# A tap table made at the start of the program, its cosine and sine rows in two partition groups

## The chip, the core and the metric

The kernel runs on one core of a Trainium2 chip. A core has a matrix engine (TensorE, PE in the profile; PEld is its loading of weights), a vector engine (VectorE, DVE), an activation engine (ScalarE, ACT), a general engine (GpSimd, POOL) and a sync engine (SyncE, SP) whose queue issues most of the transfers. Each engine runs its own instructions in order, and they meet at semaphores. The metric is device time in microseconds of one execution, the median of several runs; less is better.

## The reference

Two layers run over 256 latent tokens and 256 context tokens of width 1024. Layer 0 mixes tokens with a Conformer convolution module, layer 1 with a bidirectional mLSTM, and each is followed by an MLP with squared ReLU. The change concerns the start of layer 0:

```python
u = modulate(h, sh1, sc1)          # h * (1 + sc1) + sh1
def conformer_conv(u, rows, w_pw1, b_pw1, w_dw, b_dw, ln_g, ln_b, w_pw2, b_pw2):
    a = u @ w_pw1 + b_pw1
    a = a[..., :CONV_DIM] * jax.nn.sigmoid(a[..., CONV_DIM:])
    ...
        a = dwconv(a, w_dw)         # 31 taps, per channel
    ...
    a = jax.nn.silu(layer_norm(a + b_dw, ln_g, ln_b))
    return a @ w_pw2 + b_pw2
```

The shift `sh1` and the scale `sc1` come from `silu(c) @ ada_w + ada_b`.

## The kernel before

Features lie on the partitions in eight tiles of 128, and both token streams together are 512 columns. A large product is made of three matmuls (`mm3`, L181, L184, L185): a weight is split into a rounded part `wh` and a residual `wl`, the activation into `u` and its residual, and three of the four products are summed. The split of weights is a cast on ACT (L150) and a subtraction on DVE (L151).

**The load time.** The first eight blocks run in a loop over f. `start0(f)` loads a block of modulation weights (`raw`, 1024 KB), a tile of x (256 KB) and a piece of the first convolution weights (`F`, 256 KB), and runs eight matmuls of 32 columns each on four column tiles of PE (L343). `start1(f)` folds their four partial sums with a small matrix `fold` (L351), adds the biases out of `vecs` (L637, L638), splits the weights and makes u and its residual (L600, L601, L603). `start2(f)` runs twelve matmuls into four accumulators `ps0`. While `pin` is set, PE keeps the order of the program. Until the first loads have landed PE runs matmuls on a tile of ones (`idle`, L175): 13, then 3, then 5.

**The convolution.** The 31 taps are applied in the frequency domain: rows of a are transformed by a matmul with a table `F0`, multiplied by the taps' spectrum `Hc` and `Hs` on DVE (L867, L868) and transformed back with `G1` and `G2` (L878). The tables are angles, made of iotas on POOL, which DVE reduces and turns into sines by a polynomial of twelve steps (L704 to L713), once over 384 columns (`F0`, `G1`, `G2`) and once over 256 (`WC`, `WS`). The spectrum is `taps` (L735 to L740): four f32 matmuls of 31 rows of `WC` or `WS` with the taps, two after each of the second and third column blocks of the main product (m = 1 and 2 of `pw1_next`), each result scaled by `cf` on ACT. All of this stands in a region of lower priority (L667 to L741), so that its DVE instructions fall between those of the loop and the product.

**What sets the order.** A scheduler puts each engine's instructions in order; instructions that were issued with `keep_in_program_order` stay as they are written, and `issue_after` puts one behind another. SP issues the loads in the order of its queue: first `vecs` (204 KB), then raw, x and F of each block; a load into a tile that is still read waits in the queue, with all that stands behind it.

Of the kernel before, what the change touches and what calls it, by code (L numbers as in the profile page):

```python
# [14 lines left out]
P = 128  # L15
# [56 lines left out]
def hybrid_kernel(ctx: ExitStack, tc: tile.TileContext, xT, vecs_d, wdw_d, ada0_w, ada_w, wg_d, pw1a, pw1, pw2, w1_0, w2_0,  # L72
# [49 lines left out]
    def VA(name):  # L122
        o, w = _OFF[name]
        return vecs[:, o:o + w]

    ident = con.tile([P, P], F32, name="ident")
    make_identity(nc, ident)
    ones = con.tile([P, P], F32, name="ones")
# [8 lines left out]
    fold = con.tile([P, 16], F32, name="fold")  # L137
    nc.vector.tensor_tensor(fold, ident[:, 0:16], ident[:, 32:48], op=ALU.add)
    for j in (2, 3):
        folded = nc.vector.tensor_tensor(fold, fold, ident[:, 32 * j:32 * j + 16], op=ALU.add).ins  # L140
# [16 lines left out]
    def split_w(src, make=None):  # L157
        n = src.shape[-1]
        if make is not None:
            his, los = [], []  # L160
            for i in range(0, n, T):
                his.append(make(F32R))
                los.append(make(F32R))
                split(his[-1], los[-1], src[:, i:i + T])
            return his, los
        hi = wp.tile([P, 1024], F32R, tag="wh", name=nm("wh"), bufs=NW)[:, :n]
        lo = wp.tile([P, 1024], F32R, tag="wl", name=nm("wl"), bufs=NW)[:, :n]
        anchors.append(split(hi, lo, src))
        return hi, lo
# [3 lines left out]
    def idle(ps, n):  # L173
        for _ in range(n):
            a = nc.tensor.matmul(ps[:, 0:P], ones, ones, start=True, stop=True)  # L175
            if pin[0]:
                tc.keep_in_program_order(a)
        return a.ins
# [149 lines left out]

    cs = con.tile([P, DT, 48], F32, name="cs")
    nc.vector.memset(cs, 0.0)  # L330
    sgc = con.tile([P, 2 * DT], F32, name="sgc")
    cc = vecs[:, _OFF["c_ctx"][0]:_OFF["c_ctx"][0] + 2 * DT]
    nc.scalar.activation(sgc, cc, AF.Sigmoid)
    for i in range(2):
        nc.vector.tensor_tensor(cs[:, :, 14 + i], sgc[:, i * DT:(i + 1) * DT], cc[:, i * DT:(i + 1) * DT], op=ALU.mult)
    ada = [con.tile([P, 48, 2], F32, name=f"ada{l}") for l in range(2)]

    mark_unit = [None]
# [270 lines left out]
    F = maker(padp, "F", 5)  # L609

    x, u = [], []
    KO0 = 4
    ps0 = [psum("cv" if m == 3 else "mm") for m in range(KO0)]
    sc1 = con.tile([P, 2, DT], F32, name="sc1p")
# [3 lines left out]

    def start0(f):
        t = X()  # L620
        raw = raw_load(ada0_w[f])
        nc.sync.dma_start(t, xT[f * P:(f + 1) * P, :])
        wr = F()
        nc.sync.dma_start(wr[:, :KO0 * P], pw1a[f])
        x.append(t)
        ps = psum("fl")[:, :2 * P]
        ada_mm(ps, [raw[:, kt * 2 * P:(kt + 1) * 2 * P] for kt in range(DT)])
        sb = F()[:, :2 * P]
        with tc.issue_after(folded):
            st[f] = wr, sb, nc.vector.tensor_copy(sb, ps).ins  # L630

    def start1(f):
        with tc.issue_after(st[f][2]):
            w = split_w(st[f][0][:, 0:KO0 * P])
        tr = ada_fold(st[f][1], 2 * P, tag="ln")
        with tc.issue_after(lastsub[0]):
            nc.vector.tensor_scalar(sh1[:, :, f], tr[:, 0:2], vecs[:, o0 + f:o0 + f + 1], None, op0=ALU.add)  # L637
            nc.vector.tensor_scalar(sc1[:, :, f], tr[:, 2:4], vecs[:, o0 + DT + f:o0 + DT + f + 1], 1.0,  # L638
                                    op0=ALU.add, op1=ALU.add)
        u.append((U(F32R), U(F32R)))  # L640
        affine_split(*u[f], x[f], sc1, sh1, f)
        st[f] = w

    def start2(f, ms):
        for m in ms:
            mm3(ps0[m], *kcol(st[f], m), *u[f], f == 0, f == DT - 1)

    pin[0] = Z.pin0
# [18 lines left out]

    later = tc.high_priority(-100)
    later.__enter__()
    foldg = con.tile([P, 16], F32, name="foldg")  # L670
# [3 lines left out]
    HL = L // 2  # L674
    ij = F()
    fj, jj = ij[:, 0:L], ij[:, L:2 * L]
    pc = padp.tile([P, 8], F32, name="pc")
    exact = dict(channel_multiplier=0, allow_small_or_imprecise_dtypes=True)
# [3 lines left out]
    p_, gt, fp, p15, ph1, ph2, cf, z0 = [pc[:, i:i + 1] for i in range(8)]  # L682
    nc.gpsimd.iota(p_, [[1, 1]], base=0, channel_multiplier=1, allow_small_or_imprecise_dtypes=True)
    nc.vector.tensor_scalar(gt, p_, float(HL), None, op0=ALU.is_gt)
    nc.vector.scalar_tensor_tensor(fp, gt, -float(HL), p_, op0=ALU.mult, op1=ALU.add)
    nc.vector.tensor_scalar(p15, p_, float(NTAP // 2), None, op0=ALU.subtract)
# [3 lines left out]
    nc.vector.tensor_scalar(z0, p_, 0.0, None, op0=ALU.is_equal)  # L690
    nc.vector.tensor_scalar(cf, p_, float(HL), None, op0=ALU.is_equal)
    nc.vector.tensor_tensor(cf, cf, z0, op=ALU.add)
    nc.vector.tensor_scalar(cf, cf, -1.0 / L, 2.0 / L, op0=ALU.mult, op1=ALU.add)
    tab = padp.tile([P, 5 * L], F32, name="tab")
    F0, G1, G2, WC, WS = [tab[:, i * L:(i + 1) * L] for i in range(5)]
    nc.vector.tensor_scalar(F0, fj, p_, None, op0=ALU.mult)
    nc.vector.tensor_scalar(G1, jj, fp, ph1, op0=ALU.mult, op1=ALU.add)
    nc.vector.tensor_scalar(G2, jj, fp, ph2, op0=ALU.mult, op1=ALU.add)
    nc.vector.tensor_scalar(WC, fj, p15, None, op0=ALU.mult)
    nc.vector.tensor_scalar(WS, fj, p15, -L / 4, op0=ALU.mult, op1=ALU.add)  # L700
    nc.vector.tensor_scalar(F0[:, HL + 1:L], F0[:, HL + 1:L], -L / 4, None, op0=ALU.add)
    for t_ in (tab[:, 0:3 * L], tab[:, 3 * L:5 * L]):
        tz, sq_ = [F()[:, :t_.shape[-1]] for _ in range(2)]
        nc.vector.tensor_scalar(tz, t_, 1.0 / L, MAGIC, op0=ALU.mult, op1=ALU.add)  # L704
        nc.vector.tensor_scalar(tz, tz, MAGIC, -float(L), op0=ALU.subtract, op1=ALU.mult)
        nc.vector.tensor_tensor(t_, t_, tz, op=ALU.add)
        nc.vector.scalar_tensor_tensor(tz, t_, -1.0, t_, op0=ALU.mult, op1=ALU.max)
        nc.vector.tensor_scalar(t_, tz, -1.0, L / 4, op0=ALU.mult, op1=ALU.add)
        nc.vector.tensor_tensor(sq_, t_, t_, op=ALU.mult)
        nc.vector.tensor_scalar(tz, sq_, SIN[5], None, op0=ALU.mult)  # L710
        for k in (4, 3, 2, 1):
            nc.vector.scalar_tensor_tensor(tz, tz, SIN[k], sq_, op0=ALU.add, op1=ALU.mult)
        nc.vector.scalar_tensor_tensor(t_, tz, SIN[0], t_, op0=ALU.add, op1=ALU.mult)  # L713

    def masked(name, zero):
        t = padp.tile([P, L], F32, name=name)
# [10 lines left out]
    bdw = padp.tile([P, D], F32, name="bdw")  # L727
    nc.sync.dma_start(bdw, wdw_d[NTAP:NTAP + 1, :].broadcast_to([P, D]))
    Hc, Hs = [padp.tile([P, D], F32, name=n_) for n_ in ("Hc", "Hs")]

    wds = [tmp("L")[:NTAP, :] for _ in range(2)]
    for h_ in range(2):
        nc.sync.dma_start(wds[h_], wdw_d[0:NTAP, h_ * 512:(h_ + 1) * 512])

    def taps(h_):  # L735
        wd = wds[h_]
        for t, w_ in ((Hc, WC), (Hs, WS)):
            ps = psum("ln")
            nc.tensor.matmul(ps, w_[:NTAP, :], wd, start=True, stop=True)
            nc.scalar.activation(t[:, h_ * 512:(h_ + 1) * 512], ps, AF.Identity, scale=cf)  # L740
    later.__exit__(None, None, None)  # L741


# [185 lines left out]
    def pw1_next(m, ps):  # L929
# [27 lines left out]
        if m == 8:  # L957
            for i, tag in enumerate("SLSL"):
                half.append(tmp(tag))
                nc.sync.dma_start(half[i], ada_w[0, 6 + ada_s2.n, 0, :, i * 512:(i + 1) * 512])  # L960
        if m == 10:
            pw2_raw.extend(raw_load(pw2[g, 0]) for g in range(2))
            for i in range(4):
# [1100 lines left out]
```

## Time and profile before

| | us |
|---|---|
| three timed runs | 1659.6, 1661.2, 1662.05 |
| median | 1661.2 |
| span of the profiled execution, first to last instruction | 1658.8 |
| PE busy in it | 1647.3 |
| DVE busy | 1042.7 |
| ACT busy | 730.4 |
| mean granted PE clock | 0.998 of full |

The time of the profiled execution itself, with what lies before and after its span, isn't listed. In rows of the timeline stand the start, the length, the engine, the line, the operation with what it writes and reads, how many are merged, and in brackets how long the engine had been idle and what ended that. In rows of the chain stand the start, the length and the work: it is followed back from the last instruction, at each step to what released it. Groups by line give the busy time in all, the mean of one in ns, and the idle time ahead of them.

### The profile page before, as it was taken

The page shows a single profiled execution, that of the slowest core. Times are in us where ns is not written, and L with a number is a line of the kernel's source. Part 1 is how long each engine was busy: PE and PEld are TensorE (multiplying, and loading weights), DVE is VectorE, ACT ScalarE, POOL GpSimd, SP SyncE. Part 2 cuts the span into 40 slices and gives each one's busy share as a digit, 9 for nine tenths or more (in the row PEclk, how much of TensorE's full clock was granted, in tenths as well). Part 3 has the DMA queues.
Part 4 walks back from the last instruction along what each step waited for, and adds up shares of the span by engine and source line. Part 5 has one row for each costly group of instructions (what it writes and reads, how often), then busy time and mean ns, then how long its engine had stood idle before and what let it go on. Part 6 is the DMA issues. An engine that isn't in the chain of part 4 may idle for free.

```text
span 1658.8 us, 22681 instructions
## 1 busy us (share of the span) xinstructions
PE 1647.3 (99%) x8824; PEld 1357.0 (82%) x8824; DVE 1042.7 (63%) x1875; ACT 730.4 (44%) x1174; POOL 14.3 (1%) x64
## 2 busy tenths in 40 slices
PE   9999999999999999999999999999999999999998
PEld 7665998888888998877787899888878888878887
DVE  6564895666535776762254753563489776776677
ACT  4313572232324475652133533442478654555453
POOL 0000000000000000000000000000000000000001
PEclk9999999999999999999999999999999999999999
DMA  9666223434424066557774852554466655675552
GB/s 359 229 213 239 96 71 116 163 123 147 137 102 153 1 225 204 184 194 272 282 255 145 301 179 80 178 190 151 147 227 219 212 211 202 242 283 186 178 186 93
DMA packets 80411, 305.80 MB, mean 184 GB/s; under 512 B 11854, under 2 KB 30066, under 8 KB 50352
## 3 DMA queue, kind: packets, MB, share of 16 engines
q1 hardware_dynamic: 57840, 288.06, 49.5%
q10 hardware_dynamic: 22464, 16.30, 3.0%
q8 instruction: 69, 1.13, 0.3%
q14 instruction: 38, 0.31, 0.1%
HBM read 286.47 MB, written 17.86 MB: 183 GB/s over the span
## 4 chain that ended last, share of the span: by engine, by line
PE 93%; DVE 4%; DMA 1%; ACT 1%; issue 1%; SPq 0%; DVEq 0%; ACTq 0%
PE mm L181 17%; PE mm L184 17%; PE mm L185 17%; PE mm L196 7%; PE mm L197 4%; PE mm L212 3%; PE mm L214 3%; PE mm L213 3%; PE cv L212 2%; PE fl L343 1%; PE cv L214 1%; PE cv L213 1%; DVE wl L151 1%; PE ln L181 1%; PE cv L878 1%; PE ln L184 1%
## 5 line engine op out<-in xcount | busy, mean ns | idle before, releaser
L151 DVE TENSOR_TENSOR wl<-raw,wh 128x1024 fp32r<-128x1024 f32 x344 | 418.5, 1221 | 248.1 <-ACT wh L150 246.5
L150 ACT CAST wh<-raw 128x1024 fp32r<-128x1024 f32 x344 | 358.6, 1051 | 463.3 <-PE mm L184 245.1
L184 PE MATMUL mm<-u,wh 128*128 128x512 f32 (+1 forms) x808 | 292.2, 362 | 0.2 <-DVE u L603 0.2
L181 PE MATMUL mm<-u,wh 128*128 128x512 f32 (+1 forms) x680 | 244.1, 360 | 0.0
L185 PE MATMUL mm<-u,wl 128*128 128x512 f32 (+1 forms) x680 | 241.5, 356 | 0.0
L184 PEld LDWEIGHTS mm<-u,wh 128*128 128x128 f32 x808 | 153.0, 189 | 23.3 <-issue 1.0
L181 PEld LDWEIGHTS mm<-u,wh 128*128 128x128 f32 x680 | 128.8, 190 | 24.9 <-issue 6.3
L185 PEld LDWEIGHTS mm<-u,wl 128*128 128x128 f32 x680 | 128.8, 190 | 17.9
L212 PE MATMUL mm<-wh,xl 128*128 128x512 f32 x256 | 101.2, 395 | 0.9 <-ACT wh L150 0.8
L181 PE MATMUL mm<-xm,wh 128*128 128x512 f32 x256 | 101.0, 395 | 0.0
L213 PE MATMUL mm<-wh,xl 128*128 128x512 f32 x256 | 100.0, 391 | 0.0
L185 PE MATMUL mm<-xm,wl 128*128 128x512 f32 x256 | 99.7, 389 | 0.0
L214 PE MATMUL mm<-wl,xl 128*128 128x512 f32 x256 | 99.4, 392 | 0.1
L181 PE MATMUL mm<-hid,wh 128*128 128x512 f32 (+1 forms) x256 | 93.3, 364 | 0.0
L185 PE MATMUL mm<-hid,wl 128*128 128x512 f32 (+1 forms) x256 | 92.8, 363 | 0.0
L184 PE MATMUL mm<-hid,wh 128*128 128x512 f32 (+1 forms) x256 | 92.8, 363 | 0.0
L196 PE MATMUL mm<-x,wh 128*128 128x512 f32 x232 | 81.1, 398 | 0.0
L184 PE MATMUL mm<-qq,wh 128*128 128x272 f32 x256 | 73.9, 289 | 0.0
L181 PE MATMUL mm<-qq,wh 128*128 128x272 f32 x256 | 73.5, 288 | 0.0
L185 PE MATMUL mm<-qq,wl 128*128 128x272 f32 x256 | 73.5, 288 | 0.0
L196 PE MATMUL mm<-u,wh 128*128 128x512 f32 x192 | 68.6, 399 | 0.0
L1120 DVE SCALAR_TENSOR_TENSOR x<-mm,ada,x 128x256 f32<-128x256 f32 x64 | 28.5, 479 | 62.4 <-PE mm L185 62.4
(537 smaller groups left out, 3245.2 us busy)
## 6 DMA issues: line engine op xcount, KB each, us to landing
raw<-w SPq DMA_DIRECT2D x64, 1024.0 KB, 4.8
raw<-wo SPq DMA_DIRECT2D x32, 1024.0 KB, 5.3
raw<-ada_w SPq DMA_DIRECT2D x22, 1024.0 KB, 7.3
ar<-ada_w SPq DMA_DIRECT2D x80, 256.0 KB, 4.1
raw<-wv SPq DMA_DIRECT2D x16, 1024.0 KB, 7.3
raw<-wqT SPq DMA_DIRECT2D x16, 1024.0 KB, 5.6
raw<-wq SPq DMA_DIRECT2D x16, 1024.0 KB, 6.2
raw<-wk SPq DMA_DIRECT2D x16, 1024.0 KB, 4.8
```

What stands on the lines that cost most here:

```text
L150: c = nc.scalar.copy(hi, src)
L151: lastsub[0] = nc.vector.tensor_tensor(lo, src, hi.bitcast(F32), op=ALU.subtract).ins
L181: a = nc.tensor.matmul(ps, wh, xh, start=start, stop=False)
L184: nc.tensor.matmul(ps, wh, xl, start=False, stop=False)
L185: lastmm[0] = nc.tensor.matmul(ps, wl, xh, start=False, stop=stop).ins
L196: todo = [lambda s_, e_: nc.tensor.matmul(ps, wh, r[0], start=s_, stop=e_), lambda s_, e_: nc.tensor.matmul(ps[:, :n], wl, r[0][:, :n], st ...
L197: lambda s_, e_: nc.tensor.matmul(ps[:, :n], wl, r[0][:, :n], start=s_, stop=e_)]
L212: nc.tensor.matmul(ps, xh, wh, start=start, stop=False)
L213: nc.tensor.matmul(ps, xl, wh, start=False, stop=False)
L214: nc.tensor.matmul(ps, xh, wl, start=False, stop=stop)
L343: a = mark_unit[0] = nc.tensor.matmul(ps[32 * j:32 * j + 32], cs[:, kt, 14 - 2 * v:46 - 2 * v], blocks[kt], start=first and kt < 4, stop=l ...
L1120: nc.vector.scalar_tensor_tensor(res[m][:, sl_], p_, g[:, m:m + 1], res[m][:, sl_], op0=ALU.mult, op1=ALU.add)
```

## The change

The taps' table becomes one tile `WCS` of 128 columns: partitions 0 to 30 hold the cosines, 64 to 94 the sines, with a phase `ph1` of a quarter turn in the second group. It is made first, in a fixed order on DVE, out of iotas that now stand first on POOL. The taps are loaded twice, into partitions 0 to 30 and 64 to 94 of `bdw` (the tile that later takes the bias rows). The four matmuls become two pairs on row tiles 0 and 64: one pair ahead of the first modulation matmuls and one behind them. The idle matmuls are 9, none and 4 instead of 13, 3 and 5. `vecs` is loaded in two pieces, the first of 16 columns. The first block's weights are split behind its bias additions, no longer ahead of them. `fold`, `cf` and the other helper columns are made behind the table, and `sgc` and `cs` too. The later sine runs over 384 columns only.

```diff
-    nc.sync.dma_start(vecs, vecs_d)
+    nc.sync.dma_start(vecs[:, 0:2 * DT], vecs_d[:, 0:2 * DT])
...
+    et = tmp("E")
+    fe = et[:, 0:L]
+    nc.gpsimd.iota(p_, [[1, 1]], base=0, channel_multiplier=1, allow_small_or_imprecise_dtypes=True)
+    nc.gpsimd.iota(fe[:, 0:HL + 1], [[1, HL + 1]], base=0, **exact)
+    nc.gpsimd.iota(fe[:, HL + 1:L], [[1, HL - 1]], base=1, **exact)
...
+        for d_, s_ in ((raw, ada0_w[f]), (t, xT[f * P:(f + 1) * P, :]), (wr[:, :KO0 * P], pw1a[f])):
+            lastload[0] = tc.keep_in_program_order(nc.sync.dma_start(d_, s_)).ins
+        if f == 0:
+            tc.keep_in_program_order(nc.sync.dma_start(vecs[:, 2 * DT:], vecs_d[:, 2 * DT:]))
...
-        with tc.issue_after(st[f][2]):
-            w = split_w(st[f][0][:, 0:KO0 * P])
+        if f:
+            with tc.issue_after(st[f][2]):
+                w = split_w(st[f][0][:, 0:KO0 * P])
...
+        if f == 0:
+            with tc.issue_after(sc_.ins), tc.issue_after(tapped[0]):
+                w = split_w(st[f][0][:, 0:KO0 * P])
...
+    def sines(t_, tz, sq_, keep=lambda o: o):
+        keep(nc.vector.tensor_scalar(tz, t_, 1.0 / L, MAGIC, op0=ALU.mult, op1=ALU.add))
...
+        for k in (4, 3, 2, 1):
+            keep(nc.vector.scalar_tensor_tensor(tz, tz, SIN[k], sq_, op0=ALU.add, op1=ALU.mult))
+        return keep(nc.vector.scalar_tensor_tensor(t_, tz, SIN[0], t_, op0=ALU.add, op1=ALU.mult))
+
+    def taps(h_, pss):
+
+        for r, ps in zip((0, HL), pss):
+            r_ = slice(r, r + NTAP)
+            tc.keep_in_program_order(nc.tensor.matmul(ps, WCS[r_, :], bdw[r_, h_ * 512:(h_ + 1) * 512], start=True,
+                                                      stop=True, tile_position=(r, 0)))
+        return pss
...
+    for r in (0, HL):
+        nc.sync.dma_start(bdw[r:r + NTAP, :], wdw_d[0:NTAP, :])
...
+    keep(nc.vector.tensor_scalar(WCS, fe, p15, ph1, op0=ALU.mult, op1=ALU.add))
+    wsin = sines(WCS, et[:, L:2 * L], et[:, 2 * L:3 * L], keep)
...
-    idle(spare, 13)
+    idle(spare, 9)
+    tapped = [taps_out(0, taps(0, [ps0[2], ps0[3]]))]
     start0(0)
-    idle(spare, 3)
+    t1_ = taps(1, [psum("ln"), spare])
     start1(0)
-    idle(spare, 5)
+    taps_out(1, t1_)
+    idle(ps0[1], 4)
     start0(1)
...
-    for t_ in (tab[:, 0:3 * L], tab[:, 3 * L:5 * L]):
-        tz, sq_ = [F()[:, :t_.shape[-1]] for _ in range(2)]
...
+    sines(tab[:, 0:3 * L], *[F()[:, :3 * L] for _ in range(2)])
...
-        if m in (1, 2):
-            taps(m - 1)
```

The order of instructions on PE at the start of the program, before (`raw` are the modulation weights, `fl` their result, `cv` with `ones` the idle matmuls, `mm` the first accumulator):

```order
L175 MATMUL cv_111<-ones 128x128 x13
L343 MATMUL fl_131<-raw_126,cs 32x256 x8
L175 MATMUL cv_111<-ones 128x128 x3
L351 MATMUL ln_149<-fold,F_140 128x2 x2
L175 MATMUL cv_111<-ones 128x128 x5
L343 MATMUL fl_173<-raw_168,cs 32x256 x8
L181 MATMUL mm_105<-u_154,wh_145 128x512
```

and with the change (`bdw` are the taps, `tab` their table):

```order
L179 MATMUL cv_143<-ones 128x128 x9
L674 MATMUL mm_104<-bdw,tab 128x512
L674 MATMUL cv_105<-bdw,tab 128x512
L342 MATMUL fl_164<-raw_158,cs 32x256 x8
L674 MATMUL ln_175<-bdw,tab 128x512
L674 MATMUL cv_143<-bdw,tab 128x512
L350 MATMUL ln_178<-fold,F_173 128x2 x2
L179 MATMUL mm_103<-ones 128x128 x4
L342 MATMUL fl_207<-raw_202,cs 32x256 x8
L185 MATMUL mm_102<-u_187,wh_183 128x512
```

The two pairs of taps stand on either side of the first modulation matmuls, and 8 idle matmuls fewer follow them.

The second place is DVE at the start. With the change, behind the memset of cs and ahead of everything that start0 and start1 need of DVE, stand these rows (`pc` are helper columns, `E` a working tile):

```order
L334 MEMSET cs 128x384
L687 TENSOR_SCALAR pc<-pc 128x1
L688 SCALAR_TENSOR_TENSOR pc<-pc 128x1
L689 TENSOR_SCALAR pc<-pc 128x1
L690 TENSOR_SCALAR pc<-pc 128x1
L691 TENSOR_SCALAR tab<-E_75,pc 128x128
L659 TENSOR_SCALAR E_75<-tab 128x128
L660 TENSOR_SCALAR E_75<-E_75 128x128
L661 TENSOR_TENSOR tab<-tab,E_75 128x128
L662 SCALAR_TENSOR_TENSOR E_75<-tab 128x128
L663 TENSOR_SCALAR tab<-E_75 128x128
L664 TENSOR_TENSOR E_75<-tab 128x128
```

Six more steps of the sine follow, and only then cs, which before stood right behind its memset.

The third place is PE between the second and the third later column block of the main product, before (`ident` marks transposes):

```order
L185 MATMUL mm_681<-u_472,wl_686 128x512
L824 MATMUL ln_713<-ident,E_644 128x128 x4
L739 MATMUL ln_721<-L_575,tab 128x512
L739 MATMUL ln_724<-L_575,tab 128x512
L181 MATMUL mm_682<-u_154,wh_727 128x512
```

and with the change:

```order
L189 MATMUL mm_678<-u_506,wl_683 128x512
L342 MATMUL fl_750<-raw_746,cs 32x512
L185 MATMUL mm_679<-u_187,wh_718 128x512
L188 MATMUL mm_679<-u_188,wh_718 128x512
L851 MATMUL ln_710<-ident,E_647 128x128 x4
L189 MATMUL mm_679<-u_187,wl_719 128x512
```

The taps are gone. One of the eight modulation matmuls, which stood four and four behind this column block, now stands alone ahead of it, and three remain where four were.

More of the change, by code (lines that the diff above doesn't have):

```diff
@@ L124, in VA @@
         return vecs[:, o:o + w]
+    HL = L // 2
+    exact = dict(channel_multiplier=0, allow_small_or_imprecise_dtypes=True)
+    pc = con.tile([P, 8], F32, name="pc")
+    p_, gt, fp, p15, ph1, ph2, cf, z0 = [pc[:, i:i + 1] for i in range(8)]
+    et = tmp("E")
[3 more added lines that the diff above has]
+    nc.gpsimd.iota(fe[:, HL + 1:L], [[1, HL - 1]], base=1, **exact)
     ident = con.tile([P, P], F32, name="ident")
@@ L135, in hybrid_kernel @@
     nc.vector.memset(eps, EPS)
[L137 to L140, printed above, removed]
     def raw_load(src):
@@ L330, in hybrid_kernel @@
     nc.vector.memset(cs, 0.0)
[L331 to L335, printed above, removed]
     ada = [con.tile([P, 48, 2], F32, name=f"ada{l}") for l in range(2)]
@@ new lines, in hybrid_kernel @@
+    wsin = sines(WCS, et[:, L:2 * L], et[:, 2 * L:3 * L], keep)
+    sgc = con.tile([P, 2 * DT], F32, name="sgc")
+    cc = vecs[:, _OFF["c_ctx"][0]:_OFF["c_ctx"][0] + 2 * DT]
+    nc.scalar.activation(sgc, cc, AF.Sigmoid)
+    for i in range(2):
+        keep(nc.vector.tensor_tensor(cs[:, :, 14 + i], sgc[:, i * DT:(i + 1) * DT], cc[:, i * DT:(i + 1) * DT], op=ALU.mult))
+    with tc.issue_after(wsin.ins):
+        fold = con.tile([P, 16], F32, name="fold")
+        nc.vector.tensor_tensor(fold, ident[:, 0:16], ident[:, 32:48], op=ALU.add)
+        for j in (2, 3):
+            folded = nc.vector.tensor_tensor(fold, fold, ident[:, 32 * j:32 * j + 16], op=ALU.add).ins
@@ L669, in hybrid_kernel @@
     later.__enter__()
+    behind = tc.issue_after(wsin.ins)
+    behind.__enter__()
     foldg = con.tile([P, 16], F32, name="foldg")
@@ L726, in hybrid_kernel @@
     WIN = [[(F0[0:96, :], 0)], [(ge32, 0), (lt32, 1)], [(ge96, 0), (F0[0:96, :], 1)], [(ge32, 1)]]
[L727 to L740, printed above, removed]
+    with tc.issue_after(lastload[0]):
+        nc.sync.dma_start(bdw, wdw_d[NTAP:NTAP + 1, :].broadcast_to([P, D]))
+    behind.__exit__(None, None, None)
     later.__exit__(None, None, None)
@@ L959, in pw1_next @@
                 half.append(tmp(tag))
-                nc.sync.dma_start(half[i], ada_w[0, 6 + ada_s2.n, 0, :, i * 512:(i + 1) * 512])
+                with tc.issue_after(lastload[0]):
+                    nc.sync.dma_start(half[i], ada_w[0, 6 + ada_s2.n, 0, :, i * 512:(i + 1) * 512])
         if m == 10:
```

58 lines of the change are left out of this document (28 added, 30 removed).

## The prediction

> **What bounds the kernel now.** I began with the page: busy shares, then the chain that ended last.
>
> ```profile
> span 1658.8 us, 22681 instructions
> PE 1647.3 (99%) x8824; PEld 1357.0 (82%) x8824; DVE 1042.7 (63%) x1875; ACT 730.4 (44%) x1174; POOL 14.3 (1%) x64
> PE 93%; DVE 4%; DMA 1%; ACT 1%; issue 1%; SPq 0%; DVEq 0%; ACTq 0%
> ```
>
> TensorE (PE) is busy 99% of the span and carries 93% of the chain. So a microsecond of PE work or waiting that goes near the start should reach the end nearly whole, and work on another engine is worth something only where PE waits for it. The whole idle time of PE is 1658.8 - 1647.3 = 11.5 us, and this change touches one place in it. I looked for that place in a table of two-microsecond windows (window, then its length and, per engine, busy time and count; the last three columns are granted PE clock, DMA share and GB/s).
>
> ```profile
> 56.00:58.00 2.00, 1.86 (x9) 1.20 (x7) 1.86 (x5) 0.00 (x0) 1.75 (x8) 1.00 0.98 354
> 58.00:60.00 2.00, 1.68 (x4) 0.66 (x4) 0.93 (x2) 0.52 (x1) 0.03 (x1) 1.00 0.52 196
> 60.00:62.00 2.00, 2.00 (x6) 1.38 (x6) 0.01 (x1) 1.79 (x3) 0.00 (x0) 0.61 0.33 87
> ```
>
> Between 56 and 60 us PE is idle for 0.46 us, and then the granted clock falls to 0.61. The chain of waits shows what happens there, and the groups by line give the price of the taps.
>
> ```profile
> 57.84 0.44 DVE tab L713
> ...
> 58.32 1.98 PE ln L739 x4
> 60.30 0.58 PE mm L184
> 60.89 0.43 PE mm L185
> ...
> 63.45 0.43 PE mm L185
> ...
> 64.38 0.24 PE mm L185
> L739 PE MATMUL ln<-L,tab 31*128 31x512 f32 x8 | 4.0, 614 | 0.5 <-DVE tab L713 0.5
> ```
>
> L713 is the last step of the sine table on VectorE (DVE); L739 is the spectrum of the taps, four f32 matmuls in eight records. PE waits 0.5 us for the table, spends 4.0 us on the taps, and then runs eight matmuls slowly: one of 0.58 and seven of 0.43 us (60.89 to 63.45) against 0.24 at full clock.
>
> **What the change takes from there.** Taps 4.0 us, the wait 0.5 us, the slow stretch 7 x 0.19 + 0.34 = 1.7 us. Together **6.2 us**, all on PE. The 1.7 us belong to this profiled execution; whether each timed run has that stretch isn't shown.
>
> **What it adds at the start.** The first microseconds before, where the taps now go:
>
> ```profile
> 1.12 5.39 PE L175 MATMUL cv<-ones 128*128 128x128 f32 x26 [1.12 <-DVE ones L129]
> 6.51 1.07 PE L343 MATMUL fl<-raw,cs 128*32 128x256 f32 x16
> 8.28 0.51 PE L351 MATMUL ln<-fold,F 128*128 128x2 f32 x4
> 8.65 1.36 PE L175 MATMUL cv<-ones 128*128 128x128 f32 x10
> 9.13 0.21 DVE L638 TENSOR_SCALAR sc1p<-ln,vecs 128x2 f32<-128x2 f32 x1
> 9.38 1.09 ACT L600 ACTIVATE u<-x,sh1p,sc1p 128x256 fp32r<-128x256 f32 x2 [1.02 <-DVE sc1p L638]
> 9.40 0.72 DVE L601 TENSOR_SCALAR S<-x,sc1p,sh1p 128x256 f32<-128x256 f32 x2
> 10.29 1.07 PE L343 MATMUL fl<-raw,cs 128*32 128x256 f32 x16 [0.29 <-DMA raw<-ada_w]
> 10.55 0.69 DVE L603 TENSOR_TENSOR u<-S,u 128x512 fp32r<-128x512 f32 x1
> 11.63 0.40 PE L184 MATMUL mm<-u,wh 128*128 128x512 f32 x1
> 15.69 0.50 PE L181 MATMUL mm<-u,wh 128*128 128x512 f32 x1
> 20.09 0.50 PE L181 MATMUL mm<-u,wh 128*128 128x512 f32 x1
> ```
>
> Thirteen idle matmuls fill PE until the first weights are used at 6.51. One block later the loop runs at 20.09 - 15.69 = 4.40 us a block, PE without a pause, so what counts is when the first block's second matmul starts: 11.63 before. I follow the changed program to the same matmul.
>
> First the table. DVE is free after the memset of cs. Then it runs four 128x1 operations, one 128x128 with two column operands and the sine: four with constants, two of two tensors, six fused ones, all 128x128 and each waiting for the last.
>
> ```profile
> 1.25 0.38 DVE L330 MEMSET cs<- 128x384 f32 x1
> 12.28 0.15 DVE L693 TENSOR_SCALAR pc<-pc 128x1 f32<-128x1 f32 x1
> 38.36 0.34 DVE L697 TENSOR_SCALAR tab<-F,pc 128x128 f32<-128x128 f32 x1
> 41.78 0.35 DVE L704 TENSOR_SCALAR F<-tab 128x384 f32<-128x384 f32 x1
> 51.42 0.29 DVE L704 TENSOR_SCALAR F<-tab 128x256 f32<-128x256 f32 x1
> 55.97 1.84 DVE L712 SCALAR_TENSOR_TENSOR F<-F,F 128x256 f32<-128x256 f32 x4
> ```
>
> An operation with constants falls by 0.06 us per 128 columns, so 0.23 at 128. A fused one takes 1.84/4 = 0.46 at 256 columns; at 128 no row shows it: between 0.23 (half) and 0.46; I take 0.32. So 1.63 + 4 x 0.17 + 0.36 + 4 x 0.25 + 8 x 0.32 = **6.2 us** (5.5 to 7.4 with the bounds). The table's last step is the only thing the first taps wait for that can be late: nine idle matmuls end at 1.12 + 18 x 5.39/26 = 4.85, so PE stands **1.4 us** there with the whole program behind it. It costs nothing by itself, since the first weights are used at 6.51 anyway.
>
> Then the pair. Two row tiles at once aren't in this form before; the nearest rows are the forward pairs on 64 partitions.
>
> ```profile
> 92.75 0.62 PE ln L853
> ...
> 93.38 0.42 PE ln L853
> ```
>
> Two matmuls of 512 columns take 1.04 us there, against 1.98 for two one after the other. I take 1.04 a pair; the other end is 2.0. At full clock: taps 6.2 to 7.3, the modulation matmuls 7.3 to 8.3 (1.0), the second pair to 9.35, behind which the fold waits; its input was copied long before. From fold to sc1p it took 9.13 - 8.28 = 0.85, so sc1p starts at 10.2. Behind sc1p the subtraction that splits the first weights (0.69, like that of u at 10.55, which has its size) now stands ahead of S, so the residual u starts at 10.2 + 0.27 + 0.69 + 0.72 = 11.9 and ends at 12.6. ACT's u is sooner (10.45 + 1.09). PE needs both for the matmul of 11.63: **1.0 us later**. The loads don't set this:
>
> ```profile
> 7.00:12.00 5.00, 4.71 (x51) 3.49 (x44) 3.85 (x20) 2.27 (x4) 0.00 (x0) 1.00 1.04 429
> ```
>
> Two tap loads of 31 x 4 KB are 0.25 MB, 0.6 us at 429 GB/s, so the second block's weights come at 10.9 instead of 10.29 and their matmuls end at 11.9, below 12.6.
>
> At **half clock** PE's part is dearer: pair 2.0 instead of 1.04, modulation 2.0 instead of 1.0. Rows that speak for it: the 26 records at the start run at 5.39/26 = 0.21 us each, the ten at 8.65 at 0.136, so PE begins slowly whatever the clock column says; and at 58 us a wait of only 0.5 us followed by taps on 31 of 128 rows brought the clock to half for over 3 us. The new start has a wait of 1.4 us and then taps again. I take one slow stretch as long as that one, and 1.4 of its 1.7 us, since part of it falls on the copy and the fold, where PE waits for DVE: **2.4 us later** in place of 1.0.
>
> The Trainium skill, TensorE: Matmul & The Clock Gate, section "HAM oscillation — how this bites in real kernels", says that only PE gaps over about 3.4 us cost the clock. By that rule the 1.4 us gap is harmless and the full-clock sum would hold. The row at 58 us differs: 0.5 us of idle sufficed there, with thinly filled matmuls behind it; the measurement decides, and the rule stays a rival.
>
> **What it adds later.** Two places, from the order of instructions:
>
> ```profile
> 41.92 0.50 PE L184 MATMUL mm<-u,wh 128*128 128x512 f32 x1 [0.23 <-DVE u L603]
> 73.31 1.00 PE fl L343 x8
> ```
>
> At 41.92 PE waited 0.23 us for the last block's u. Now two 384-wide steps of the sine (0.35 each) stand ahead of u where two small ones were: **0.3 us** more. At 73.31 four modulation matmuls ran side by side on four column tiles in 1.00 us. Now the first of them stands alone, ahead of the matmuls of the next column block, and the other three follow where the four were. One f32 matmul of 512 columns is half of 1.98, so **1.0 us** more, and 0.2 for the change of tile shape (0.43 for a first matmul after it, against 0.24). Between 0 and 1.2; I take 1.2, since neither neighbour can fill the other columns.
>
> What is hidden: the smaller sine table on DVE later (it had no one waiting but the taps), Hc and Hs on ACT at the start (the first two lie beside the modulation matmuls, the second two ahead of block 1's cast and beside block 0's 4.40 us of PE; without that cover block 1 is late by what they take), the vector columns loaded in two pieces, the bias rows, which come later but are first used behind the inverse transforms.
>
> **Sum.** Against the profiled execution: 6.2 - 2.4 - 0.3 - 1.2 = **2.3 us** gained at a slow start, 6.2 - 1.0 - 0.3 - 1.2 = **3.7 us** at full clock. That execution's own time isn't listed; its span is 0.8 to 3.3 us below the three runs and 2.4 below their median, so I put it at the median, 1661.2. A run of before without the slow stretch would have 1.7 us less to gain.
>
> **The rivals.**
>
> A, the forecast: slow start. 1661.2 - 2.3 = **1658.9**. For it: the slow first records and 58 us. Chance 0.5.
>
> B, full clock at the start (also the skill's rule above): 1661.2 - 3.7 = 1657.5, and 1656.3 if the lone matmul overlaps its neighbours. For it: nine idle matmuls are 3.7 us of full work ahead of the gap. Against: the gap is thrice that at 58 us. Chance 0.38.
>
> C, the other side: the two row tiles don't run together, 2.0 us a pair, and at half clock 4.0. Then taps to 10.2, modulation to 12.2, second pair to 14.2 or 16.2, 4.8 to 6.8 us behind the 9.35 of above, so block 0 is 5.8 to 7.8 us late in place of 1.0. With the 1.5 us added later it is slower than before from a delay of 6.2 - 1.5 = 4.7 us on: 1662.3 to 1664.3, and up to 1666.0 where before has no slow stretch. For it: 31-row tiles at rows 0 and 64 appear nowhere before. Against: the 64-row pair overlapped. Chance 0.12.
>
> **How the numbers follow.** A measurement of this kernel can tell about 0.2% from no change: 3.3 us, so "faster" means under 1657.9 and "slower" over 1664.5. B lies just beyond the line, so does a part of A (0.05), while a part of B (0.03) falls short: faster 0.40. C reaches the upper line only where before has no slow stretch: slower 0.08. The rest, 0.52, is no change. The range: B with a cheap lone matmul and a table at 5.5 us gives 1655.6; A with a table at 7.4 gives 1660.1, and with no slow stretch in before 1661.8. C is left out, and little else.
>
> **What would show it.** Right: PE at the start waits 1 to 2 us for tab and taps; each pair of row tiles takes about 1.1 us, or 2 when slow; the second matmul of block 0 starts at 12.4 to 14.2; nothing waits for tab near 58 us and the clock is full from 56 to 64; the lone modulation matmul costs about 1 us. Wrong: a slow stretch that moves elsewhere, a table much later than 6.2, pairs of 2 us at full clock, or block 1 waiting for its cast behind Hc and Hs on ACT.

## The result, and the profile after

| | before | after |
|---|---|---|
| timed runs (five each) | 1658.9 to 1662.05 us | 1670.64 to 1671.64 us |
| median | 1660.86 us | 1671.29 us |
| span of the profiled execution | 1658.8 us | 1669.8 us |
| PE busy in it | 1647.3 us | 1649.8 us |
| mean granted PE clock | 0.998 | 0.992 |

After over before is 1.0068, 95% interval 1.0057 to 1.0079: **10.4 us slower**, where 2.3 us faster was forecast. The profiled execution after took 1671.51 us, 1.7 more than its span. All that follows goes by spans.

PE's waits come first, since PE was busy 99% of the span before (what waited, for whom; total, times, longest, in us):

```profile
PE mm L674 <- DMA bdw<-wdw_d: 6.3, 1, 6.3
PE cv L674 <- DMA bdw<-wdw_d: 3.1, 1, 3.1
PE cv L179 <- DVE ones L138: 1.1, 1, 1.1
PE fl L342 <- DMA raw<-ada_w: 0.5, 1, 0.5
PE mm L188 <- DVE u L602: 0.4, 1, 0.4
```

L674 are the tap matmuls. The first pair doesn't wait for the table, as forecast, but for `bdw`, the tile that the two tap loads fill: 6.3 and 3.1 us. No wait for `tab` is left near 58 us. The two row tiles of the first pair (`mm` and `cv`) don't even run side by side: the second starts when its own copy of the taps has landed. The timeline of after puts these waits in their places:

```profile
1.12 4.21 PE L179 MATMUL cv<-ones 128*128 128x128 f32 x18 [1.12 <-DVE ones L138]
1.26 0.62 SPq L686 DMA_DIRECT2D bdw<-wdw_d  x2
6.38 0.29 DVE L668 SCALAR_TENSOR_TENSOR tab<-E,tab 128x128 f32<-128x128 f32 x1
11.62 2.04 PE L674 MATMUL mm<-bdw,tab 31*128 31x512 f32 x2 [6.29 <-DMA bdw<-wdw_d]
16.80 2.07 PE L674 MATMUL cv<-bdw,tab 31*128 31x512 f32 x2 [3.14 <-DMA bdw<-wdw_d]
19.40 1.94 PE L342 MATMUL fl<-raw,cs 128*32 128x256 f32 x16 [0.53 <-DMA raw<-ada_w]
28.59 0.63 PE L188 MATMUL mm<-u,wh 128*128 128x512 f32 x1
```

The idle matmuls end at 5.33 and the table is ready at 6.38 + 0.29 = 6.67. But the first copy of the taps, issued at 1.26, is used at 11.62 and the second at 16.80, 5.2 us after it. The first modulation weights, which were used at 6.51 before, come at 19.40. The last row is the matmul on which the prediction put its sum, the second of block 0: 28.59 instead of 11.63, **17.0 us later** where 1.0 to 2.4 were forecast.

The windows of two microseconds show how the loads ran meanwhile (the last three columns are clock, DMA share and GB/s):

```profile
8.00:10.00 2.00, 0.00 (x0) 0.00 (x0) 0.36 (x3) 0.00 (x0) 0.00 (x0) 0.74 1.07 379
10.00:12.00 2.00, 0.38 (x1) 0.41 (x2) 0.00 (x0) 0.00 (x0) 0.00 (x0) 0.50 0.90 304
12.00:14.00 2.00, 1.66 (x2) 0.09 (x1) 0.00 (x0) 0.30 (x1) 0.00 (x0) 0.50 0.56 157
14.00:16.00 2.00, 0.00 (x0) 0.00 (x0) 0.00 (x0) 0.38 (x1) 0.00 (x0) 0.50 0.06 25
16.00:18.00 2.00, 1.20 (x2) 0.50 (x2) 0.00 (x0) 0.00 (x0) 0.00 (x0) 0.50 0.31 55
...
28.00:30.00 2.00, 2.00 (x12) 1.72 (x9) 1.04 (x3) 0.00 (x0) 0.00 (x0) 0.64 0.50 89
30.00:32.00 2.00, 2.00 (x9) 1.40 (x8) 1.57 (x5) 1.60 (x3) 0.00 (x0) 1.00 0.94 397
```

The row that matters is 14 to 16 us: a DMA share of 0.06 is one sixteenth, 25 GB/s. That is one of the 16 DMA engines at work and fifteen with nothing to do, in the part of the program that lives on loads. A load of 124 KB at 25 GB/s takes 5.0 us, about the distance from 11.62 to 16.80. PE has been idle since 5.33 when its clock falls, and from about 9 to 29 us it is at half, which makes the little work there slower as well (the first modulation matmuls take 1.94 us instead of 1.07).

So the first theory was **T1**: a load of 31 rows is moved by one DMA engine, at 25 GB/s, and that engine's share of the big loads queues behind it, so that these end late too. The rivals were **T2**, that the place of the two loads ahead of the weights costs the time, with whatever row count, and **T3**, that it is the table and the half clock on PE.

### The profile page after: what moved, and what is told of

The parts are those of the page before. It is cut to its first block, busy times and chain, and to the rows that moved or that the text cites. A ratio compares the mean times of both kernels' runs of the same rounds, so it can differ in the third digit from the quotient of the medians.

```text
span 1669.8 us, 22652 instructions
## 1 busy us (share of the span) xinstructions
PE 1649.8 (99%) x8808; PEld 1355.8 (81%) x8808; DVE 1042.6 (62%) x1877; ACT 729.4 (44%) x1174; POOL 14.4 (1%) x66
## 3 DMA queue, kind: packets, MB, share of 16 engines
q10 hardware_dynamic: 22464, 16.30, 3.1%
## 4 chain that ended last, share of the span: by engine, by line
PE 96%; DVE 2%; DMA 1%; issue 0%; ACT 0%; SPq 0%; DVEq 0%; ACTq 0%
PE mm L185 18%; PE mm L188 17%; PE mm L189 17%; PE mm L200 7%; PE mm L216 4%; PE mm L218 4%; PE mm L217 4%; PE mm L201 4%; PE fl L342 2%; PE cv L216 2%; PE cv L218 2%; PE cv L217 2%; DMA raw<-ada_w 1%; PE ln L185 1%; PE cv L905 1%; PE ln L188 1%
```

## The experiments

Every ratio is to runs of the kernel before on the same chip; their medians lay between 1659.7 and 1660.1 us in the four groups of runs. Diffs are cut to the lines that matter.

**Rows of the tap loads.** One row more a load: row 31 of the source exists, and no matmul reads it in the tile.

```diff
-        nc.sync.dma_start(bdw[r:r + NTAP, :], wdw_d[0:NTAP, :])
+        nc.sync.dma_start(bdw[r:r + NTAP + 1, :], wdw_d[0:NTAP + 1, :])
```

> The changed kernel, but each of the two tap loads takes 32 rows (the 31 taps and the bias row behind them) in place of 31; the matmuls still read 31. Theory 1, one DMA engine moves a 31-row load: near 15 us of the changed kernel only one sixteenth of the DMA engines is busy, at 25 GB/s, and 124 KB at 25 GB/s are 5 us for each load, with shares of the big loads queued behind them. With 32 rows both loads land before 6 us, PE waits for the table until about 6.6 us, and the time is 1656 to 1660. Theory 2, the place of the loads ahead of the big ones and their few rows: 32 rows change nothing, 1669 to 1672. Theory 3, table and half clock on PE, the loads being late only by the way: over 1667.

Measured: **1660.3 us**, ratio 1.0002 (0.9993 to 1.0011), 0.3 above the 1656 to 1660 that T1 expected and far below the 1667 and more of T2 and T3. The 32nd row takes off 11.0 us.

The same two loads put into the kernel before, where nobody reads them, once with 31 rows and once with 32 (SP issues them behind `vecs`):

```diff
+    bdw = padp.tile([P, D], F32, name="bdw")
+    for r in (0, 64):
+        nc.sync.dma_start(bdw[r:r + 31, :], wdw_d[0:31, :])
```

> The kernel before, with the two 31-row tap loads of the change added behind the load of vecs; nothing reads them before the bias rows overwrite that tile. Theory 1: the first block's modulation weights share one engine with 248 KB that stand ahead of them, so they land about 10 us late and the time is 6 to 12 us over before. Theory 2: the same, and e3 too. Theory 3: at most 1 us over before, since no instruction waits for the added loads.

> As e2, with 32 rows in each added load. Theory 1: 256 KB more at 429 GB/s, 0 to 1 us over before. Theory 2: as e2, 6 us or more. Theory 3: 0 to 1 us.

Measured with 31 rows: 1676.7 us, ratio 1.0101 (1.0087 to 1.0115); with 32 rows: 1661.96, ratio 1.0012 (1.0003 to 1.0021). Without a table or taps at the start, the 31-row loads alone cost 16.8 us; T1 had the sign and undersized it. 16.8 less the 6.2 forecast as gain is 10.6, against the change's 10.4; that they agree so well is partly luck, since 1.25 us of later costs and 1.4 us won back near the end, both below, are left out. The 32-row loads cost 2.0, more than the 0 to 1 of T1 and far less than the 6 of T2. PE's first row behind the idle matmuls, with 31 and then with 32 rows:

```profile
20.15 1.93 PE L343 MATMUL fl<-raw,cs 128*32 128x256 f32 x16 [13.87 <-DMA raw<-ada_w]
```

```profile
8.21 1.07 PE L343 MATMUL fl<-raw,cs 128*32 128x256 f32 x16 [1.41 <-DMA raw<-ada_w]
11.90 1.07 PE L343 MATMUL fl<-raw,cs 128*32 128x256 f32 x16 [0.19 <-DMA raw<-ada_w]
```

6.51 became 20.15 with 31 rows: the first weights, which have nothing to do with the taps, arrive 13.6 us late. The single packets in the trace show why, and why T1's 10 us were too few. Each tap load of 31 rows is 31 packets of 4 KB, and the 62 of them follow one another, each starting where the one before ends: from 2.82 to 17.14 us here, from 2.18 to 16.30 in the changed kernel. Right behind the last one, again one after the other, come 8 KB packets of the weights. A packet of 4 KB took 0.16 us when nothing else ran (25 GB/s) but 0.23 us in the mean of the 62, so the pair took 14.3 us and not 10. With 32 rows the 64 packets overlap and are done between 2.57 and 5.03 us. There the first weights come 1.7 us late, and the second block's 1.6 (11.90 against 10.29).

Last, the rows of the change cut in two, 16 and 15, so that no row is added:

```diff
-        nc.sync.dma_start(bdw[r:r + NTAP, :], wdw_d[0:NTAP, :])
+        for i_ in (0, 16):
+            n_ = min(16, NTAP - i_)
+            nc.sync.dma_start(bdw[r + i_:r + i_ + n_, :], wdw_d[i_:i_ + n_, :])
```

> The changed kernel with each 31-row tap load cut into one of 16 and one of 15 rows: the same bytes in the same place, four issues in place of two. Theory 1: within 1.5 us of e1 (two more issues on SP ahead of the first big load, 0.4 us each). Theory 2: as the changed kernel or later. Theory 3: as e1, both over 1667.

Measured: 1659.97 us, ratio 1.0002 (0.9993 to 1.0011), within the 1.5 us of e1_rows32 that T1 expected. T1 stands. T2 accounts for some 2 us of the 12.7 between forecast and result, by the kernel before with 32-row loads; T3 falls as the cause: the kernel with the 31-row loads and no table at the start is as late. The Trainium skill, DMA: Bandwidth & Descriptors, section "🔬 Why a DMA increments its semaphore by 16 and not by 1", says that a copy is given the largest number of engines, up to 16, that divides its slowest dimension. By that rule 31 rows get one engine, 32 and 16 get sixteen and 15 get fifteen; the share of 0.06 at 25 GB/s, the 62 packets in one line and these four kernels agree.

**Why the change doesn't gain without the defect.** The change with 32 rows should have brought the 2.3 to 3.7 us of the forecast, and its median brought none. Its profile, one execution of 1655.92 us, shows the forecast's start nearly as it was drawn:

```profile
6.73 0.69 PE L674 MATMUL mm<-bdw,tab 31*128 31x512 f32 x1 [1.40 <-DVE tab L668]
6.73 0.69 PE L674 MATMUL cv<-bdw,tab 31*128 31x512 f32 x1
...
7.79 1.07 PE L342 MATMUL fl<-raw,cs 128*32 128x256 f32 x16
...
11.88 1.07 PE L342 MATMUL fl<-raw,cs 128*32 128x256 f32 x16 [0.43 <-DMA raw<-ada_w]
12.88 0.50 PE L185 MATMUL mm<-u,wh 128*128 128x512 f32 x1
13.22 0.40 PE L188 MATMUL mm<-u,wh 128*128 128x512 f32 x1
```

PE waits 1.40 us for the table, and the pair of row tiles takes 7.79 - 6.73 = 1.06 us. Block 0's second matmul comes at 13.22, 1.6 us later than before. What holds it is the second block's weights at 11.88, 1.6 late, as in the kernel before with the same two loads; u isn't waited for, since its residual is ready at 12.87, near the 12.6 that the prediction worked out. Other executions of the same kernel went to 1661.31, and in six of eleven the mean clock was 0.997 or less. Three theories stood for that: **L**, the loads, still set back by 1.6 us; **K**, the clock, which falls to half after the 1.4 us wait in a part of the runs; **M**, the lone modulation matmul. One edit each, to the kernel of e1_rows32:

```diff
-        nc.sync.dma_start(bdw[r:r + NTAP + 1, :], wdw_d[0:NTAP + 1, :])
+        nc.scalar.dma_start(bdw[r:r + NTAP + 1, :], wdw_d[0:NTAP + 1, :])
```

> The kernel of e1_rows32 (32 rows a tap load) with both tap loads issued by ACT instead of SP. With the 31 rows gone, three theories for why e1_rows32 (1660.3) is not 2 to 4 us faster than before. L: the tap loads still set back the first weights: SP issues them for 0.9 us ahead of the first weight load, and their bytes come first. K: the 1.4 us wait for the table and the thin taps bring PE to half clock in a part of the runs. M: the lone modulation matmul near 63 us. Here L expects the first weight load to be issued 0.9 us sooner, the second block's modulation matmuls at about 11.0 instead of 11.88, and 0.9 us less: 1659.4. K and M expect no change: 1660.3.

```diff
-    idle(spare, 9)
+    idle(spare, 13)
```

> The kernel of e1_rows32 with 13 idle matmuls ahead of the taps instead of 9, so that PE is busy until the table is ready. K expects a full clock from the start in every run (mean granted clock 0.998 or more) and 1.5 to 3 us less: 1657.3 to 1658.8. L and M expect no change: 1660.3.

Of the eight idle matmuls that the change leaves out, four stood ahead of the first weights; these come back here.

```diff
         if m == 3:
             first.extend(ada_load(0, 4))
-            ada_g1.mm(first, range(4))
+            with tc.issue_after(lastmm[0]):
+                ada_g1.mm(first, range(4))
```

> The kernel of e1_rows32 with the lone modulation matmul put back beside its three neighbours. M expects 1.0 us less, 1659.3, and the four in about 1.06 us; were the lone one hidden, no change. L and K expect no change: 1660.3.

And one that moves the taps to where PE ran idle matmuls anyway, with the tap loads behind the first block's. The split of the first block's weights also goes back ahead of its bias additions:

```diff
-    idle(spare, 9)
-    tapped = [taps_out(0, taps(0, [ps0[2], ps0[3]]))]
+    idle(spare, 13)
     start0(0)
-    t1_ = taps(1, [psum("ln"), spare])
+    idle(spare, 3)
     start1(0)
-    taps_out(1, t1_)
-    idle(ps0[1], 4)
+    taps_out(0, taps(0, [ps0[2], ps0[3]]))
+    taps_out(1, taps(1, [psum("ln"), spare]))
     start0(1)
```

> The kernel of e1_rows32 with the two tap loads issued behind the first block's three loads, the taps in place of the ten idle matmuls behind the first fold, 13 idle matmuls at the start, and cs and fold in the middle of the table. Takes away both what L and what K name: first weights used at 6.5 as in the kernel before, first block's second matmul at 11.7 to 12.4, clock full. L expects about 1.0 to 1.5 us less than e1_rows32 (1659), K 1.5 to 3 (1657.3 to 1658.8), both together 1656 to 1657.5, M alone 1660.3.

| kernel | median, us | ratio (interval) | runs at a clock under 0.998 |
|---|---|---|---|
| e1_rows32 | 1660.3 | 1.0002 (0.9993 to 1.0011) | 6 of 11 |
| e5_actqueue | 1658.47 | 0.9989 (0.998 to 0.9997) | 3 of 11 |
| e6_idle13 | 1657.32 | 0.9989 (0.998 to 0.9998) | 1 of 11 |
| e7_four | 1659.15 | 0.9995 (0.9986 to 1.0004) | 5 of 11 |
| e8_behind | 1658.75 | 0.9992 (0.9983 to 1.0001) | 4 of 11 |

By the medians the steps are twice what was expected for L (1.8 for 0.9), and as expected for K (3.0 for 1.5 to 3) and M (1.15 for 1.0); by the means they are 1.7, 1.7 and 0.6. The intervals overlap, so none is shown by its time alone, and e1_rows32 ran on another chip than the other four (their runs of before have medians of 1659.94 and 1659.97). That the wait brings the lower clock is supported by the counts: with the wait filled only one run is left under 0.998. That the lower clock is what keeps e1_rows32 from gaining isn't shown: its five runs at 0.999 average 1659.3 us, its six others 1660.1. What the half clock costs at the start is seen in the execution of e5_actqueue that was profiled:

```profile
6.59 0.69 PE L674 MATMUL mm<-bdw,tab 31*128 31x512 f32 x1 [1.34 <-DVE tab L668]
...
8.78 1.22 PE L674 MATMUL ln<-bdw,tab 31*128 31x512 f32 x1
...
15.76 0.40 PE L188 MATMUL mm<-u,wh 128*128 128x512 f32 x1
```

The clock falls between the two pairs (0.69 and 1.22 us a record), and block 0's second matmul comes at 15.76. e8_behind missed its 1656 to 1657.5: the second block's weights still came at 11.94, where PE waited 0.98 us for them, right behind the taps, and the first block's second matmul came at 13.27 instead of 11.7 to 12.4. 4 of its 11 runs are under 0.998; whether this wait is the reason isn't shown, since the clock was full in the profiled execution. Two questions, whether the three add up and what holds the weights, went into the next kernels.

> e5_actqueue, e6_idle13 and e7_four in one kernel: 32 rows a tap load, issued by ACT, 13 idle matmuls, four modulation matmuls together. If L, K and M each hold for about what they showed (0.7, 1.7 and 0.6 us in the means against e1_rows32's mean of 1659.75), the mean is 1656.7 and the clock full at the start in nearly every run; the first block's second matmul at 12.2 to 12.6. If the three share one cause, or the wait on the late weight load near 1407 us takes the gain back, 1657.5 to 1658.

This kernel is the edits of e5_actqueue, e6_idle13 and e7_four together. Measured: **1655.98 us**, mean 1656.22, ratio 0.9977 (0.9968 to 0.9986). All eleven runs lie between 1655.7 and 1657.22, at a clock of 0.998 or 0.999. The expectation of 1656.7 took L for 0.7 us in the means, but the runs give 1.7 (1659.75 to 1658.02). With that the three make 4.05 and 1655.7; 3.5 of it came. Its start:

```profile
6.59 0.69 PE L674 MATMUL mm<-bdw,tab 31*128 31x512 f32 x1 [0.67 <-DVE tab L668]
...
11.75 1.07 PE L342 MATMUL fl<-raw,cs 128*32 128x256 f32 x16 [0.44 <-DMA raw<-ada_w]
12.76 0.50 PE L185 MATMUL mm<-u,wh 128*128 128x512 f32 x1
13.09 0.40 PE L188 MATMUL mm<-u,wh 128*128 128x512 f32 x1
```

With the same loads and a full clock the second matmul stands at 13.09, later than the 12.2 to 12.6 expected; 15.76 in e5_actqueue is 2.7 us behind it, the cost of the half clock there. But 11.75 for the second block's weights is only 0.1 better than 11.88, where L expected 0.9. So these profiles don't bear out L's account, that SP's issue time ahead of them is what costs, and what made the runs of e5_actqueue faster is open. Next, half the bytes, in the kernel of e8_behind with the edit of e7_four:

```diff
-            for r in (0, HL):
-                tc.keep_in_program_order(nc.sync.dma_start(bdw[r:r + NTAP + 1, :], wdw_d[0:NTAP + 1, :]))
+            tc.keep_in_program_order(nc.sync.dma_start(bdw[0:NTAP + 1, :], wdw_d[0:NTAP + 1, :]))
+            for h_ in range(2):
+                c_ = slice(h_ * 512, (h_ + 1) * 512)
+                tc.keep_in_program_order(nc.scalar.copy(bdw[HL:HL + NTAP + 1, c_], bdw[0:NTAP + 1, c_]))
```

> e8_behind with one tap load of 32 rows instead of two, its second copy made on the chip by ACT, and with the four modulation matmuls of e7_four together. If the bytes and the issue of the tap loads are what set the second block's weights back (they came at 11.94 against 10.29 in the kernel before), halving them brings these to about 11.1, and 0.8 us for that and 0.6 to 1.0 for the four come off e8_behind: 1657.0 to 1657.4. If the place in the queue is all that counts, its modulation matmuls stay near 11.9 and only the four help: 1657.8 to 1658.2.

Measured: 1655.73 us, ratio 0.9979 (0.997 to 0.9988). The time is better than either account expected, but the weights came at 11.59, a gain of 0.35 for the 0.8 of the first account. What was left of the change around the loads was the split of the vector columns, undone in the next:

```diff
-    nc.sync.dma_start(vecs[:, 0:2 * DT], vecs_d[:, 0:2 * DT])
+    nc.sync.dma_start(vecs, vecs_d)
...
-            tc.keep_in_program_order(nc.sync.dma_start(vecs[:, 2 * DT:], vecs_d[:, 2 * DT:]))
```

> e10_one_load with the vector columns loaded whole and first, as in the kernel before, instead of 8 KB first and 196 KB behind the first block's loads. In the first 10 us the loads of e10_one_load moved 2.72 MB, those of the kernel before 3.06. If the split (128 rows of 64 bytes ahead, 128 short rows among the weights) is what lowers that, the second block's modulation matmuls start at about 11.0 instead of 11.6 and the median falls by 0.6 to 1655.1. If it is the tap load alone, they stay near 11.6, the first weights come 0.3 to 0.5 us later, and nothing is gained: 1655.7 to 1656.2.

Measured: **1655.15 us** over eight runs, ratio 0.9972 (0.9961 to 0.9982), the lowest median here. The windows of the first 10 us, of e10_one_load and then of this kernel, and its second block:

```profile
0.00:10.00 10.00, 8.88 (x57) 7.77 (x59) 7.62 (x37) 6.83 (x14) 2.74 (x15) 1.00 0.78 272
```

```profile
0.00:10.00 10.00, 8.88 (x59) 7.54 (x60) 7.84 (x37) 7.11 (x15) 2.85 (x15) 1.00 0.82 301
```

```profile
10.90 1.07 PE L342 MATMUL fl<-raw,cs 128*32 128x256 f32 x16
```

272 became 301 GB/s, the weights came at 10.90 instead of 11.59, and the median fell by 0.58, all as expected if the split is what lowers the rate. It isn't shown, though. The times of the two kernels overlap, and with two tap loads ahead of the weights the split made no difference: 11.90 with the vector columns whole (the kernel before with 32 rows) and 11.88 with them split (e1_rows32). The next kernel adds a third reason.

> e10_one_load with the second sine table held behind the last block's u on DVE. Undoes the term that the prediction put at 0.3 us: the wait for u near 43 us was 0.4 in every profile of the changed kernel against 0.23 before. If the two 384-wide steps are its whole cause, the wait falls to 0.2 or less and 0.2 to 0.4 us are gained, 1655.3 to 1655.5, hardly more than the measurement can tell; if something else is late there, it stays at 0.4.

`lastu` is the residual of the last block's u.

```diff
-    sines(tab[:, 0:3 * L], *[F()[:, :3 * L] for _ in range(2)])
+    with tc.issue_after(lastu[0]):
+        sines(tab[:, 0:3 * L], *[F()[:, :3 * L] for _ in range(2)])
```

Measured: 1656.6 us, ratio 0.9983 (0.9974 to 0.9992). The wait is back at what it was before:

```profile
44.54 0.50 PE L188 MATMUL mm<-u,wh 128*128 128x512 f32 x1 [0.23 <-DVE u L602]
```

It stood at 0.40 or 0.41 in the other profiles of changed kernels, so the sine steps are its cause, and they cost 0.17 us. The time doesn't show it: the median is 0.9 us above e10_one_load instead of 0.2 to 0.4 below. The start of this kernel has the same loads as e10_one_load, and yet in its profiled execution the first weights came at 7.10 instead of 6.57 and the second block's at 12.71 instead of 11.59:

```profile
0.00:10.00 10.00, 7.00 (x53) 6.22 (x54) 6.56 (x32) 5.64 (x12) 2.74 (x15) 1.00 0.77 249
```

```profile
12.71 1.07 PE L342 MATMUL fl<-raw,cs 128*32 128x256 f32 x16 [0.25 <-DMA raw<-ada_w]
```

So two executions with the same loads differ by 1.1 us and by 23 GB/s, more than e10_one_load and e11_vecs_whole in the weights (0.7 us) and nearly as much in the rate (29 GB/s). Neither the 0.35 us of the halved bytes nor the 0.7 us of the split can be told from that.

## Why the prediction was wrong, step by step

**The step that failed** is the sentence "The loads don't set this", with its working, two tap loads "are 0.25 MB, 0.6 us at 429 GB/s". It priced two small loads by their bytes at the rate of all engines, a rate taken from a window full of 128-row loads. The loads of 31 rows went one after the other through one DMA engine, at 25 GB/s at best, and a share of the first weights behind them. In place of 0.6 us they cost 16.8 in the kernel before. "The table's last step is the only thing the first taps wait for that can be late" fell with it. No rival had a late load as its mechanism; C, the only slow one, ended at 1664.3, or 1666.0 at the most.

**The rate was wrong even for whole rows.** With 32 rows the second block's weights came 1.6 us later instead of 0.6. What makes up the 1.6 wasn't found. The vector columns "loaded in two pieces" stood in the list of what is hidden; whether they are is open.

**The gains: right.** Taps, wait and slow stretch of 58 to 64 us are gone; the clock of after is 1.00 in every window from 56 to 80 us. The sum can be tested on the kernel with 32 rows, by the first forward pair (L853 before, L880 with the change), in the timelines of before, of e1_rows32 and of after:

```profile
92.68 0.69 PE L853 MATMUL ln<-A,tab 64*128 64x512 f32 x1
```

```profile
89.44 0.69 PE L880 MATMUL ln<-A,tab 64*128 64x512 f32 x1
```

```profile
105.24 0.69 PE L880 MATMUL ln<-A,tab 64*128 64x512 f32 x1
```

1.6 (start) + 0.2 (u) + 1.05 (lone matmul) - 6.2 = -3.35 us; measured 89.44 - 92.68 = -3.24. For after, 17.0 in place of 1.6 gives 12.05; measured 12.56, and in the window from 28 to 30 us the clock was still at 0.64, which slows the matmuls behind the one at 28.59.

**The table: right in kind**, 6.67 for 6.2. Its first 128-wide step took 0.81 us instead of 0.36. Where the loads let it, PE waited 1.4 us, as worked out.

**The pair: right**, 1.06 us for 1.04; at half clock 2.0 (8.78 to 10.78 in e5_actqueue). Rival C's mechanism, row tiles one after the other, didn't happen where both copies of the taps were there; in after the first pair ran so, but because the second copy was late.

**The half clock: right in kind, too cheap.** It was put at 1.4 us beyond the full clock's sum; 15.76 - 13.09 says 2.7. It isn't there in each run: by the mean clock 6 of 11 with the wait, 1 of 11 with the wait filled. A and B, which the prediction held as two cases, are two kinds of runs of one kernel. The rule cited in the prediction from the Trainium skill, TensorE: Matmul & The Clock Gate, that only gaps of over about 3.4 us cost the clock, doesn't hold here: in three of the four profiled executions with this wait (e4_rows16_15, e5_actqueue and e7_four, 1.34 to 1.89 us; not e1_rows32, 1.40) the clock fell to half behind it. What share the thin matmuls have in that wasn't separated from the gap. In the profiled executions of e3_before_32 and e12_sine_later a gap of 1.41 and 1.42 us stood ahead of modulation matmuls on all 128 rows, and the clock stayed full, which speaks for such a share but is no test of it.

**The later terms.** The wait for u was mis-sized, 0.17 us for 0.3. The lone modulation matmul took 1.05 us for 1.2, and put back, the median fell by 1.15 (the mean by 0.6). It alone, in e1_rows32, and then its three neighbours:

```profile
62.92 1.05 PE L342 MATMUL fl<-raw,cs 128*32 128x512 f32 x2
...
70.01 1.06 PE L342 MATMUL fl<-raw,cs 128*32 128x512 f32 x6
```

**From there to the end.** By the span after is 11.0 us late, not 12.56. The rows of one group of matmuls (duration ns, then the first and the last start) in before, after, e1_rows32 and e9_all_three show the stretch in which 1.4 us went:

```profile
L212 PE MATMUL mm<-wh,xl x256: 388/389/793, 1195.0 to 1420.7; 128*128 128x512 f32 x128
```

```profile
L216 PE MATMUL mm<-wh,xl x256: 387/389/793, 1207.2 to 1431.5; 128*128 128x512 f32 x128
```

```profile
L216 PE MATMUL mm<-wh,xl x256: 387/389/793, 1191.7 to 1415.9; 128*128 128x512 f32 x128
```

```profile
L216 PE MATMUL mm<-wh,xl x256: 387/389/793, 1190.0 to 1416.0; 128*128 128x512 f32 x128
```

From first to last it is 225.7 us in before and 226.0 in e9_all_three, but 224.3 and 224.2 in after and e1_rows32. Inside the longer ones PE waits 0.8 us (before) and 1.1 us (e9_all_three) for a weight cast (of `wh`, near 1407 us) whose load had landed late; the rest of the difference wasn't placed. The wait in before:

```profile
1409.98 0.50 PE L212 MATMUL mm<-wh,xl 128*128 128x512 f32 x1 [0.78 <-ACT wh L150]
```

So after got 1.4 us back, and e1_rows32, 3.24 us ahead at the first pair, ended 4.6 ahead: before had lost 1.4 us in this stretch and they had not. The prediction, which took a microsecond near the start to reach the end nearly whole, had no term for this.

**What stays open.** Runs of e1_rows32 at the same mean clock of 0.999 lie between 1655.92 and 1661.07. The profiles show two things that vary between executions, the landing of the second block's weights (1.1 us with the same loads) and the stretch with the wait near 1407 (up to 1.8 us); they don't add up to 5 us, and only the execution of 1655.92 us has a profile. So why the change with 32 rows brings nothing in the median is open in the main. Why the spread is only 1.5 us in e9_all_three wasn't found either, nor what share each of its three edits has in its 3.7 us under before.

## What to carry to other kernels

Price a small load by how many DMA engines can take part in it, not by its bytes: look at its row count, and whether any load of the trace has the same. 31 rows cost 16.8 us where 32 cost 2.0, and most of it fell on other loads that queued behind. Where the start of a kernel lives on loads, a load put ahead of the first weights counts even with 32 rows. A wait of PE there is better filled with idle matmuls than left open: with it filled 1 run of 11 was at a lower clock instead of 6.

## What was not expected of the hardware

A load on one engine holds up loads that use all sixteen: with two 31-row loads ahead, the first 1024 KB were used 13.6 us later, although the other fifteen engines stood idle at the end (25 GB/s, share 0.06). Packets of 4 KB on that engine took 0.16 us when nothing else ran and 0.23 us in the mean, so that the pair took 14.3 us. A PE wait of 1.3 to 1.9 us, ahead of matmuls on 31 of 128 rows, was followed by half clock in three of four profiled executions (the clock was 0.61 in the window from 8 to 10 us and 0.50 from 10 to 14 in the one of e5_actqueue). Two executions with the same loads at the start moved 2.72 and 2.49 MB in their first 10 us (e10_one_load and e12_sine_later), and the second block's weights were used 1.1 us apart.
